# A two-layer hybrid trunk: weight sums by adding transfers, weights in blocks, adaptive sums in smaller steps

## The chip, the cores and the metric

The kernel runs on one core of a Trainium2 chip: five engines with queues of their own (TensorE, here PE, with its weight loads PEld; VectorE, DVE; ScalarE, ACT; GpSimd, POOL; SyncE, SP, which before issues every transfer) and 16 DMA engines that all transfers share. The metric is the device time of one execution in microseconds (us), as the median of several runs.

## The reference

A decoder trunk of two layers on a sequence of 1024 rows of 1024 features, then a final RMSNorm, all in float32:

```python
for l in range(DEPTH):                      # 2
    ada = c_act @ w_ada[l] + b_ada[l]       # 1024 -> 3072
    shift, scale, gate = jnp.split(ada, 3, axis=-1)
    h = rmsnorm(x, norm_g[l]) * (1.0 + scale[:, None, :]) + shift[:, None, :]
    p = h @ w_in[l]                         # 1024 -> 9224: mq, mk, mv, mo, mz, mi, mf, rq, rk, rv, rz
    ...
    cell = mlstm_chunkwise(mq_c, mk_c, mv, mi + b_igate[l], mf + b_fgate[l])      # 4 heads of 256
    y_m = jax.nn.sigmoid(mo) * head_layernorm(cell, gn_m[l], 4) * jax.nn.silu(mz)
    ret = retention_chunkwise(rq_h, rk_h, rv)                                      # 4 heads of 256
    y_r = head_layernorm(ret, gn_r[l], 4) * jax.nn.silu(rz)
    x = x + gate[:, None, :] * (jnp.concatenate([y_m, y_r], axis=-1) @ w_out[l])
return rmsnorm(x, final_g)
```

The adaptive row `ada` depends on the conditioning vector alone. The projection `h @ w_in` is most of the work.

## The kernel before

Each layer goes through a border stage (adaptive gains, the normalised input in transposed form, the first column blocks, gate logits and values of head 0), a stage of four mLSTM heads, a stage of four retention heads, and the output projection. In the trace layer 0's heads lie at about 100 to 850 us, layer 1's at 1150 to 1900.

Every float32 product is made of three products in a faster 32-bit form: a matrix is split into a high part (`hH`, `wH`: a cast) and a low part (`hL`, `wL`: the matrix less its high part), and `mm3` (line 688) multiplies high by high, low by high and high by low. `split` (line 911) does this for a 128x512 weight tile: a cast, mostly on ScalarE, then a subtraction on VectorE.

The projection goes two column blocks of 128 at a time (`pair`, line 934; 34 pairs a layer). Each block is halved along the 1024 input features, and the input along features and time, so a pair is a product of 2x2 matrices of halves; it is made with seven products of halves in place of eight (Strassen and Winograd's way). For that, sums of halves of the input are made once a layer (`sums_of_input`, line 1438, the forms T1 to T4), and sums of halves of the weights for each pair: with `a11, a21, a22, a12` the four 256 KB weight tiles, VectorE makes four sums of 128x512 in `pair`. A product of halves (`product`, line 918) is four times three matmuls of 128x512. The last product of a pair is carried into the next (`finish_pair`, line 925).

Weight tiles (`raw`, named `s` for the first sum) live in 6 slots `R0` to `R5` and up to 4 shared ones (`raw_slots`, line 796); their split halves (`wH`, `wL`) in 9 slots. A tile is overwritten only when its last reader is done, so a load, a sum and a split wait for each other through the slots. `block` (line 906) loads a tile on SyncE's queue; in DRAM the rows of 128 columns that it wants lie apart, so it comes in runs of 512 bytes.

The adaptive rows of later use (layer 1's shift and scale, both layers' gates) are made by jobs beside the pairs: `ada_rows` (line 780) loads eight tiles of 128x512 and adds them up on VectorE, each times a value of the conditioning vector (`aacc <- araw, cact`). A job is a generator, advanced by one step after each pair from a given pair on (line 1733); before, a step takes a whole row of eight loads.

The order of all instructions on all engines is fixed when the program is built: a list scheduler (`Program`, line 204) records every operation and places them by its own table of costs, due times and slots, and line 1892 then issues them in that order. This is why nearly every row of the profile has the line L1892 and groups are told apart by tile names. Each engine runs its queue strictly in this order, and a waiting instruction holds all behind it.

Of the kernel before, what the change touches and what calls it, by code (L numbers as in the profile page):

```python
# [3 lines left out]

# [1 line left out]

# [10 lines left out]
ALU = mybir.AluOpType  # L17
# [3 lines left out]
P = 128  # L21
# [590 lines left out]


@with_exitstack
def tile_hybrid_trunk(ctx, tc, x, xt, c, positions, w_ada, b_ada, norm_g, w_in, conv_w, conv_b,
                      b_igate, b_fgate, gn_m, gn_r, w_out, final_g, consts, out):
    nc = tc.nc
    x = x[0]
# [50 lines left out]
    def bank(cls):  # L669
        return new(cls, 512, "p" + cls)  # L670
# [107 lines left out]
                V.scalar_tensor_tensor(acc, raw, cact[:, kk:kk + 1], acc, ALU.mult, ALU.add)  # L778

    def ada_rows(l, c0):  # L780
        acc = new("raw", 512, "aacc", slots=raw_slots())
        raws = []
        for k in range(KT):
            raw = new("raw", 512, "araw", slots=raw_slots())
            Q.dma_start(raw, w_ada[l, k * P:(k + 1) * P, c0:c0 + 512])
            raws.append(raw)
        ada_acc(acc, raws)
        return acc

    def column_sums(pt, acc, at=0):  # L790
# [5 lines left out]
    def raw_slots():  # L796
        return R_TAGS + E_TAGS[0:{"border": 1, "ml": 4, "ret": 0}[phase[0]]]

    def ada_column_job(l, half):
        part = small("adap", 4, "s2")  # L800
        yield
        acc = ada_rows(l, half * 512)
        pt = bank("p")
        column_sums(pt, acc)
        V.tensor_copy(part, pt[:, 0:4])
        yield
        acc = ada_rows(l, D + half * 512)
        pt = bank("p")
        column_sums(pt, acc)
        finish_gsh(l, half * 4, 4, part, pt[:, 0:4])  # L810

    def gate_col_job(l):
        for half in range(2):
            acc = ada_rows(l, 2 * D + half * 512)
# [4 lines left out]
            yield  # L819

    def gate_row_job(l):
        for half in range(2):
            acc = ada_rows(l, 2 * D + half * 512)
# [12 lines left out]
            Q.dma_start(gbdr[half], g)  # L836
            yield
# [73 lines left out]
    def split(src):  # L911
# [6 lines left out]
    def product(pt, w, form, first, last):  # L918
        for k in range(4):
            cs = slice(k * P, (k + 1) * P)  # L920
            mm3(pt, (w[0][:, cs], w[1][:, cs]), forms[form][k], first and k == 0, last and k == 3, skip_group_check=True)

    carried = [None]

    def finish_pair():
        if carried[0] is None:
            return
        pX, a22, x2, done = carried[0]
        carried[0] = None
        product(pX, split(a22), "T4", False, True)  # L930
        copy(x2[0], pX)
        done()

    def pair(c1, c2, lead, done1, done2, last=False):
        a11, a21, a22 = block(c1, 0), block(c2, 0), block(c2, 1)
        s1 = new("raw", 512, "s1", slots=raw_slots())
        pX, pW = bank("p"), None
        product(pX, split(a11), "B11", True, True)
        a = new("c", 512, "ca")
        copy(a, pX)  # L940
        V.tensor_tensor(s1, a21, a22, ALU.add)
# [24 lines left out]

        def p7():
            product(pX, w3, "T3", False, True)
            x2 = new("X", W_X, "x")
            h2 = [x2[:, lead + i * HALF:lead + (i + 1) * HALF].part(i) for i in range(2)]  # L970
            V.tensor_tensor(h2[1], pX, c, ALU.add)
            carried[0] = (pX, a22, h2, lambda: done2(x2))

        if last:
            p7()
            p3()
            finish_pair()
        else:
            p3()
            p7()  # L980
# [457 lines left out]
    def sums_of_input(hf):  # L1438
        def cut(name, srcs):
            forms[name] = []  # L1440
            for s in srcs:
                two = pair_of()
                split_to(two, s)
                forms[name].append(two)

        for k in range(4):
            combine(hf[k][0], hf[k][1], hf[k][0], ALU.subtract)
        cut("T1", [hf[k][0] for k in range(4)])
        for k in range(4):
            combine(hf[k][1], hf[k][1], hf[4 + k][1], ALU.subtract)  # L1450
        for k in range(4):
            combine(hf[4 + k][1], hf[4 + k][1], hf[k][0], ALU.subtract)
        cut("T2", [hf[4 + k][1] for k in range(4)])
        cut("T3", [hf[k][1] for k in range(4)])
        for k in range(4):
            combine(hf[4 + k][0], hf[4 + k][0], hf[4 + k][1], ALU.subtract)
        cut("T4", [hf[4 + k][0] for k in range(4)])

    def plain_forms():
# [10 lines left out]
    def logit_weights(l):  # L1470
        gr = new("c", 64, "gr")
        Q.dma_start(gr.rearrange("p (k g) -> p k g", k=KT),
                    w_in[l, :, OFF_I:OFF_I + 8].rearrange("(k p) g -> p k g", p=P))
        return gr

    def value_weights(l, gr, res, k2s):
        for k2 in k2s:
            raw = new("raw", 512, "vraw", slots=raw_slots())
            Q.dma_start(raw.rearrange("p (a b) -> p a b", a=2),
                        w_in[l, k2 * 2 * P:(k2 + 1) * 2 * P, OFF_MV:OFF_MV + HD].rearrange("(a p) b -> p a b", p=P))  # L1480
            for a in range(2):
                k = 2 * k2 + a
                w = new("vw", HD + 8, "vwH", F32R), new("vw", HD + 8, "vwL", F32R)
                split_to([t[:, 0:HD].part("v") for t in w], raw[:, a * HD:(a + 1) * HD])
                split_to([t[:, HD:].part("g") for t in w], gr[:, k * 8:(k + 1) * 8])
                res.append(w)

# [216 lines left out]
    for l in range(DEPTH):  # L1704
# [186 lines left out]
    for op in made:  # L1891
# [3 lines left out]
ROUNDS = 8  # L1895
REPORT = None

_INS = ['x', 'xt', 'c', 'positions', 'w_ada', 'b_ada', 'norm_g', 'w_in', 'conv_w', 'conv_b', 'b_igate', 'b_fgate',
        'gn_m', 'gn_r', 'w_out', 'final_g']

_OUTS = [((1, T, D), 'float32')]
# [24 lines left out]
```

## Time and profile before

| | us |
|---|---|
| median of 3 runs | 2122.83 (2121.16 to 2123.99) |
| the profiled execution: its own time | 2123.29 |
| its span in the trace | 2121.4 |
| TensorE busy in it | 2091.6 (99%) |
| VectorE, ScalarE, GpSimd busy | 1769.5, 1096.8, 111.5 |
| bytes moved by DMA | 360.93 MB, DMA share 60.9% |

Names are the program's tiles without buffer numbers; `out<-in` says what an instruction writes and reads. In rows of groups stand count, busy time, mean ns of one, and the idle time of the engine before them with what ended it. In rows of waits stand the sum, the number and the longest. In rows of the timeline stand start and length, and in brackets the idle time ahead with what ended it. A matmul's end is modelled and overlaps the next one's start, so its length is not its cost. The windows give, for a stretch of time, each engine's busy time and count, the granted clock, the share of time that the DMA engines moved data, and GB/s.

### The profile page before, as it was taken

The numbers are of one execution on the slowest core, as the hardware profiler recorded it, in microseconds if no ns is written. First come the engines' busy times: TensorE is split into PE (matmuls) and PEld (weight loads), VectorE is DVE, ScalarE is ACT, GpSimd is POOL, SyncE is SP. The second block draws the span as 40 slices with busy tenths as digits, with TensorE's granted clock in tenths as the row PEclk, the third lists the DMA queues.
The fourth block names the chain that finished last, engine by engine and source line by source line (L and its number), as shares of the span: only waits on it lengthen the run. The fifth ranks groups of instructions, "written<-read, shape, count | busy, mean of one in ns | idle before, by whom it ended". The sixth has DMA issues, their size and how long they took to land.

```text
span 2121.4 us, 30466 instructions
## 1 busy us (share of the span) xinstructions
PE 2091.6 (99%) x10013; PEld 1743.0 (82%) x10013; DVE 1769.5 (83%) x3386; ACT 1096.8 (52%) x2017; POOL 111.5 (5%) x150
## 2 busy tenths in 40 slices
PE   6999999999999999999999999999999999999998
PEld 5888888888888888888888888888888888888886
DVE  7999999898988878867679998888998778788564
ACT  6754656566343434544556566555554444445342
POOL 0010111100000000000000010000000000000000
PEclk8999999999999999999999999999999999999999
DMA  9236476457585855978433665465666565679783
GB/s 296 69 109 162 129 188 174 123 143 188 171 232 152 217 142 146 267 259 267 160 96 84 156 160 153 111 166 130 186 173 167 121 176 133 159 208 275 215 246 98
DMA packets 552554, 360.93 MB, mean 170 GB/s; under 512 B 225203, under 2 KB 483003, under 8 KB 552397
## 3 DMA queue, kind: packets, MB, share of 16 engines
q1 hardware_dynamic: 552396, 359.00, 60.9%
q8 instruction: 79, 1.29, 0.3%
q14 instruction: 79, 0.64, 0.1%
HBM read 252.43 MB, written 106.46 MB: 169 GB/s over the span
## 4 chain that ended last, share of the span: by engine, by line
PE 88%; DVE 6%; DMA 2%; issue 1%; SPq 1%; ACT 1%; POOL 0%; POOLq 0%; DVEq 0%; ACTq 0%
PE pp L1892 66%; PE pa L1892 22%; DVE x L1892 1%; DVE wL L1892 1%; SPq L1892 1%; DMA araw<-in_w_ada_dram 1%; DVE rt L1892 1%; DVE acc L1892 1%; DMA vdr<-vt 0%; DVE raw L1892 0%; DVE st L1892 0%; DMA gdr<-x 0%; DMA vraw<-in_w_in_dram 0%; DMA qdr<-x 0%; ACT sq L1892 0%
## 5 line engine op out<-in xcount | busy, mean ns | idle before, releaser
L1892 PE MATMUL pp<-hH,wH 128*128 128x512 f32 x1968 | 780.8, 397 | 4.5 <-ACT hH L1892 3.1
L1892 PE MATMUL pp<-hH,wL 128*128 128x512 f32 x1968 | 779.2, 396 | 0.7 <-DVE wL L1892 0.7
L1892 PE MATMUL pp<-hL,wH 128*128 128x512 f32 x1968 | 778.5, 396 | 1.0 <-DVE hL L1892 1.0
L1892 PEld LDWEIGHTS pp<-hH,wH 128*128 128x128 f32 x1968 | 370.3, 188 | 84.7 <-ACT hH L1892 3.1
L1892 PEld LDWEIGHTS pp<-hH,wL 128*128 128x128 f32 x1968 | 370.1, 188 | 84.7 <-DVE wL L1892 2.3
L1892 PEld LDWEIGHTS pp<-hL,wH 128*128 128x128 f32 x1968 | 370.2, 188 | 81.5 <-DVE hL L1892 1.5
L1892 ACT CAST wH<-raw 128x512 fp32r<-128x512 f32 x411 | 251.8, 618 | 350.4 <-PE pp L1892 260.4
L1892 DVE TENSOR_TENSOR wL<-raw,wH 128x512 fp32r<-128x512 f32 x416 | 283.5, 683 | 73.3 <-PE pp L1892 63.3
L1892 DVE TENSOR_TENSOR oL<-wo,oH 128x512 fp32r<-128x512 f32 x128 | 87.8, 686 | 99.2 <-PE pa L1892 36.1
L1892 ACT CAST oH<-wo 128x512 fp32r<-128x512 f32 x128 | 79.3, 619 | 137.0 <-PE pp L1892 60.4
L1892 DVE SCALAR_TENSOR_TENSOR acc<-x,cols,acc 128x1024 f32<-128x1024 f32 x96 | 122.4, 1275 | 4.9 <-ACT acc L1892 4.7
L1892 POOL TENSOR_TENSOR rsd<-va,mhalf 128x2 f32<-128x2 f32 x64 | 59.7, 932 | 1185.4 <-DVE va L1892 953.0
L1892 PE MATMUL pa<-cf,q 128*128 128x258 f32 (+1 forms) x384 | 104.7, 380 | 0.1
L1892 ACT ACTIVATE nd<-nd,nmu,rsd 128x256 f32<-128x256 f32 x119 | 66.2, 595 | 62.8 <-DVE nmu L1892 62.2
L1892 DVE TENSOR_TENSOR raw<-raw,raw 128x512 f32<-128x512 f32 x136 | 92.3, 681 | 0.6
L1892 PEld LDWEIGHTS pa<-q,kk 128*128 128x128 f32 x512 | 75.0, 191 | 8.1 <-ACT nd L1892 0.7
L1892 PE MATMUL pa<-q,kk 128*128 128x128 f32 (+1 forms) x512 | 79.5, 301 | 0.5 <-ACT nd L1892 0.5
L1892 PEld LDWEIGHTS pa<-cf,q 128*128 128x128 f32 x384 | 69.6, 189 | 11.6 <-PE pp L1892 0.5
L1892 ACT COPY ca<-pp 128x512 f32<-128x512 f32 x68 | 39.7, 583 | 73.9 <-PE pp L1892 73.8
L1892 ACT COPY cb<-pp 128x512 f32<-128x512 f32 x67 | 39.1, 584 | 60.0 <-PE pp L1892 59.4
L1892 ACT ACTIVATE yH<-yg,cols 128x512 fp32r<-128x512 f32 x64 | 46.1, 724 | 42.7 <-DVE yg L1892 41.3
L1892 PE MATMUL pa<-v,sd 128*128 128x258 f32 (+1 forms) x160 | 63.0, 394 | 0.0
(250 smaller groups left out, 3694.7 us busy)
## 6 DMA issues: line engine op xcount, KB each, us to landing
raw<-in_w_in_dram SPq DMA_DIRECT2D x280, 256.0 KB
wo<-in_w_out_dram SPq DMA_DIRECT2D x128, 256.0 KB
araw<-in_w_ada_dram SPq DMA_DIRECT2D x96, 256.0 KB
qdr<-acc SPq DMA_DIRECT2D x32, 512.0 KB
kk<-qdr SPq DMA_DIRECT2D x64, 256.0 KB
q<-qdr SPq DMA_DIRECT2D x64, 256.0 KB
ndr<-zt SPq DMA_DIRECT2D x128, 128.0 KB
qdr<-x SPq DMA_DIRECT2D x32, 512.0 KB
```

What stands on the lines that cost most here:

```text
L1892: getattr(engines[op.eng], op.fn)(*[real(v) for v in op.a], **{n: real(v) for n, v in op.k.items()})
```

## The change

Four things change. The weights `w_in` are handed over in another layout, in which each 128-column block's half lies in DRAM as one 128x512 piece (rows of 2 KB), with the eight gate columns apart as `w_gate`. The four sums of a pair are made by transfers that add the incoming block onto the tile that is there (`block_added`), issued by GpSimd; each block of the sums is so read from DRAM again. For this the signs in the seven products are set anew, so that all weight sums are plain additions: the forms of the input in `sums_of_input` and three results take the signs. And the adaptive sums give way after every four loads, start with the fifth pair (layer 0) and the seventh (layer 1), and run one after another.

```diff
     def ada_rows(l, c0):
-        acc = new("raw", 512, "aacc", slots=raw_slots())
-        raws = []
+        acc = new("raw", 512, "aacc", slots=R_TAGS)
         for k in range(KT):
             raw = new("raw", 512, "araw", slots=raw_slots())
             Q.dma_start(raw, w_ada[l, k * P:(k + 1) * P, c0:c0 + 512])
-            raws.append(raw)
-        ada_acc(acc, raws)
+            if k:
+                V.scalar_tensor_tensor(acc, raw, cact[:, k:k + 1], acc, ALU.mult, ALU.add)
+            else:
+                V.tensor_scalar(acc, raw, cact[:, 0:1], None, ALU.mult)
+            if k % 4 == 3:
+                yield
         return acc
...
     def halves(col, h):
-        return w_cur[0][h * HALF:(h + 1) * HALF, col:col + P].rearrange("(a p) b -> p a b", p=P)
+        return w_cur[0][(col if col < OFF_I else col - 8) // P, h]
...
     def block(col, h):
         raw = new("raw", 512, "raw", slots=raw_slots())
-        Q.dma_start(raw.rearrange("p (a b) -> p a b", a=4), halves(col, h))
+        Q.dma_start(raw, halves(col, h))
         return raw
...
+    def block_added(raw, col, h):
+        G.dma_start(raw, halves(col, h), accum_op=ALU.add)
+        return split(raw)
...
         product(pX, split(a22), "T4", False, True)
-        copy(x2[0], pX)
+        scaled(x2[0], pX, -1.0)
         done()
 
     def pair(c1, c2, lead, done1, done2, last=False):
         a11, a21, a22 = block(c1, 0), block(c2, 0), block(c2, 1)
-        s1 = new("raw", 512, "s1", slots=raw_slots())
-        pX, pW = bank("p"), None
+        pX = bank("p")
         product(pX, split(a11), "B11", True, True)
         a = new("c", 512, "ca")
         copy(a, pX)
-        V.tensor_tensor(s1, a21, a22, ALU.add)
         pW = bank("p")
-        product(pW, split(s1), "T1", True, True)
+        product(pW, block_added(a21, c2, 1), "T1", True, True)
         c = new("c", 512, "cc")
         copy(c, pW)
         finish_pair()
-        V.tensor_tensor(a21, a21, a11, ALU.subtract)
-        V.tensor_tensor(a11, s1, a11, ALU.subtract)
-        product(pX, split(a11), "T2", False, True)
+        product(pX, block_added(a21, c1, 0), "T2", False, True)
...
-        V.tensor_tensor(a12, a12, a11, ALU.subtract)
-        w4 = split(a12)
-        w3 = split(a21)
+        w4 = block_added(a21, c1, 1)
+        w3 = block_added(a11, c2, 0)
...
-            V.tensor_tensor(h2[1], pX, c, ALU.add)
+            V.scalar_tensor_tensor(h2[1], pX, -1.0, c, ALU.mult, ALU.subtract)
...
         if l == 0:
-            jobs += [(2, rotary_job()), (18, ada_column_job(1, 0)), (21, ada_column_job(1, 1)), (26, gate_col_job(0))]
+            jobs += [(2, rotary_job()), (5, chain(ada_column_job(1, 0), ada_column_job(1, 1), gate_col_job(0)))]
         else:
-            jobs += [(18, gate_row_job(1))]
+            jobs += [(7, gate_row_job(1))]
```

Not shown: `value_weights` and `logit_weights` read the new layout, and `kernel` makes it on the host from the inputs.

The scheduler places everything anew. Three places show how. GpSimd's queue, at the turn of layer 1's mLSTM and retention heads, before (`rsd` are reciprocal roots of an attention step, `dm` its masks):

```order
L1892 AFFINE_SELECT dm_16035<-dm_16035 128x256
L1892 AFFINE_SELECT dm_16035<-dm_16035 128x128
L1892 TENSOR_TENSOR rsd_16300<-va_16290,mhalf_72 128x2
L1892 TENSOR_TENSOR rsd_16524<-va_16517,mhalf_72 128x2
L1892 TENSOR_TENSOR rsd_16644<-va_16622,mhalf_72 128x2
```

and of the change, at the same place:

```order
L1895 AFFINE_SELECT dm_16056<-dm_16056 128x128
L1895 DMA raw_15803<-in_w_in_dram 128x512
L1895 DMA raw_15872<-in_w_in_dram 128x512
L1895 TENSOR_TENSOR rsd_16383<-va_16376,mhalf_72 128x2
L1895 DMA raw_16354<-in_w_in_dram 128x512
L1895 DMA raw_15872<-in_w_in_dram 128x512
L1895 TENSOR_TENSOR rsd_16460<-va_16453,mhalf_72 128x2
L1895 DMA raw_16202<-in_w_in_dram 128x512
L1895 DMA raw_16354<-in_w_in_dram 128x512 x2
```

The adding transfers now stand between the roots. The tile raw_16354 is added to three times, and between two of these its split must have been read. ScalarE's queue a little later, before (a cast to `wH` begins a split; `ca`, `cb`, `cc` and `x` are results copied out):

```order
L1892 CAST wH_16678<-raw_16496 128x512
L1892 ACTIVATE nd_16557<-nd_16557,nmu_16672,rsd_16644 128x256
L1892 CAST wH_16688<-raw_16398 128x512
L1892 COPY cc_16694<-pp_16654 128x512
L1892 CAST wH_16713<-raw_16585 128x512
L1892 COPY x_16636<-pp_16372 128x512
L1892 COPY cb_16737<-pp_16627 128x512
L1892 CAST wH_16744<-s_3737_16717 128x512
```

and of the change:

```order
L1895 CAST wH_16489<-raw_16202 128x512
L1895 ACTIVATE x_16409<-pp_16004 128x512
L1895 COPY cb_16518<-pp_16403 128x512
L1895 CAST wH_16524<-raw_16354 128x512
L1895 CAST wH_16540<-raw_16080 128x512
L1895 CAST wH_16581<-raw_16354 128x512
L1895 CAST wH_16588<-raw_16476 128x512
L1895 COPY ca_16612<-pp_16584 128x512
L1895 COPY cc_16628<-pp_16610 128x512
L1895 CAST wH_16633<-raw_16354 128x512
```

The casts of sums made on VectorE (`s`) are gone; three casts read one tile, each after another transfer. VectorE's queue in layer 0: an adaptive sum (`aacc`) before stands among the rotations of the retention heads (`rx`, `rot`):

```order
L1892 SCALAR_TENSOR_TENSOR aacc_6240<-araw_6253,cact_102,aacc_6240 128x512
L1892 TENSOR_TENSOR x_6211<-x_6211,rot_5065 128x512
L1892 SCALAR_TENSOR_TENSOR aacc_6240<-araw_6270,cact_102,aacc_6240 128x512
L1892 TENSOR_TENSOR x_6211<-x_6211,rx_6200 128x1024
L1892 SCALAR_TENSOR_TENSOR aacc_6240<-araw_6286,cact_102,aacc_6240 128x512
L1892 STREAM_TRANSPOSE rx_6200<-x_6211 128x6x4x32
L1892 SCALAR_TENSOR_TENSOR aacc_6240<-araw_6292,cact_102,aacc_6240 128x512
```

and now stands, wider apart, among the convolutions (`acc`) of the mLSTM heads:

```order
L1895 SCALAR_TENSOR_TENSOR aacc_2183<-araw_2425,cact_102,aacc_2183 128x512
L1895 SCALAR_TENSOR_TENSOR acc_2391<-x_2041,acc_2391 128x1024
L1895 TENSOR_TENSOR wL_2477<-raw_2290,wH_2446 128x512
L1895 STREAM_TRANSPOSE x_2041<-acc_2391 128x6x4x32
L1895 SCALAR_TENSOR_TENSOR acc_2475<-x_2296,cols_104_268,acc_2475 128x1024
L1895 SCALAR_TENSOR_TENSOR aacc_2183<-araw_2430,cact_102,aacc_2183 128x512
L1895 TENSOR_TENSOR wL_2511<-raw_2299,wH_2498 128x512
```

The number of matmuls and of SyncE's transfers is the same as before; GpSimd issues 272 transfers more, and VectorE has 272 sums less.

More of the change, by code (lines that the diff above doesn't have):

```diff
@@ L3 @@
 from contextlib import ExitStack
+from itertools import chain
 import numpy as np
@@ L614, in tile_hybrid_trunk @@
 @with_exitstack
-def tile_hybrid_trunk(ctx, tc, x, xt, c, positions, w_ada, b_ada, norm_g, w_in, conv_w, conv_b,
+def tile_hybrid_trunk(ctx, tc, x, xt, c, positions, w_ada, b_ada, norm_g, w_in, w_gate, conv_w, conv_b,
                       b_igate, b_fgate, gn_m, gn_r, w_out, final_g, consts, out):
@@ L801, in ada_column_job @@
         yield
-        acc = ada_rows(l, half * 512)
+        acc = yield from ada_rows(l, half * 512)
         pt = bank("p")
@@ L806, in ada_column_job @@
         yield
-        acc = ada_rows(l, D + half * 512)
+        acc = yield from ada_rows(l, D + half * 512)
         pt = bank("p")
@@ L813, in gate_col_job @@
         for half in range(2):
-            acc = ada_rows(l, 2 * D + half * 512)
+            acc = yield from ada_rows(l, 2 * D + half * 512)
             pt = bank("p")
@@ L818, in gate_col_job @@
                             cols[l][0][:, 120 + 4 * half:124 + 4 * half].part("a"), ALU.add)
-            yield
     def gate_row_job(l):
         for half in range(2):
-            acc = ada_rows(l, 2 * D + half * 512)
+            acc = yield from ada_rows(l, 2 * D + half * 512)
             brow = new("c", 512, "brow")
@@ L836, in gate_row_job @@
             Q.dma_start(gbdr[half], g)
-            yield
     def copy(dst, src, wait=1.0):
@@ L1446, in sums_of_input @@
         for k in range(4):
-            combine(hf[k][0], hf[k][1], hf[k][0], ALU.subtract)
+            V.tensor_tensor(hf[k][0], hf[k][0], hf[k][1], ALU.subtract)
         cut("T1", [hf[k][0] for k in range(4)])
         for k in range(4):
-            combine(hf[k][1], hf[k][1], hf[4 + k][1], ALU.subtract)
+            V.tensor_tensor(hf[k][1], hf[4 + k][1], hf[k][1], ALU.subtract)
         for k in range(4):
-            combine(hf[4 + k][1], hf[4 + k][1], hf[k][0], ALU.subtract)
+            V.scalar_tensor_tensor(hf[4 + k][1], hf[4 + k][1], -1.0, hf[k][0], ALU.mult, ALU.subtract)
         cut("T2", [hf[4 + k][1] for k in range(4)])
@@ L1455, in sums_of_input @@
         for k in range(4):
-            combine(hf[4 + k][0], hf[4 + k][0], hf[4 + k][1], ALU.subtract)
+            V.scalar_tensor_tensor(hf[4 + k][0], hf[4 + k][0], -1.0, hf[4 + k][1], ALU.mult, ALU.subtract)
         cut("T4", [hf[4 + k][0] for k in range(4)])
@@ L1472, in logit_weights @@
         Q.dma_start(gr.rearrange("p (k g) -> p k g", k=KT),
-                    w_in[l, :, OFF_I:OFF_I + 8].rearrange("(k p) g -> p k g", p=P))
+                    w_gate[l].rearrange("(k p) g -> p k g", p=P))
         return gr
@@ L1478, in value_weights @@
             raw = new("raw", 512, "vraw", slots=raw_slots())
-            Q.dma_start(raw.rearrange("p (a b) -> p a b", a=2),
-                        w_in[l, k2 * 2 * P:(k2 + 1) * 2 * P, OFF_MV:OFF_MV + HD].rearrange("(a p) b -> p a b", p=P))
+            c = slice((k2 % 2) * 256, (k2 % 2 + 1) * 256)
+            Q.dma_start(raw.rearrange("p (m b) -> p m b", m=2),
+                        w_in[l, OFF_MV // P:OFF_MV // P + 2, k2 // 2].rearrange("m p b -> p m b")[:, :, c])
+            by_row = raw.rearrange("p (m a b) -> p a m b", m=2, a=2)
             for a in range(2):
@@ L1483, in value_weights @@
                 w = new("vw", HD + 8, "vwH", F32R), new("vw", HD + 8, "vwL", F32R)
-                split_to([t[:, 0:HD].part("v") for t in w], raw[:, a * HD:(a + 1) * HD])
+                split_to([t[:, 0:HD].part("v").rearrange("p (m b) -> p m b", m=2) for t in w], by_row[:, a])
                 split_to([t[:, HD:].part("g") for t in w], gr[:, k * 8:(k + 1) * 8])
@@ L1896 @@
 REPORT = None
-_INS = ['x', 'xt', 'c', 'positions', 'w_ada', 'b_ada', 'norm_g', 'w_in', 'conv_w', 'conv_b', 'b_igate', 'b_fgate',
+_INS = ['x', 'xt', 'c', 'positions', 'w_ada', 'b_ada', 'norm_g', 'w_in', 'w_gate', 'conv_w', 'conv_b', 'b_igate', 'b_fgate',
         'gn_m', 'gn_r', 'w_out', 'final_g']
@@ L1910 @@
     arrays, args = {}, []
+    w = inputs['w_in']
+    tiles = _np.concatenate([w[:, :, :OFF_I], w[:, :, OFF_I + 8:]], axis=2).reshape(DEPTH, 2, 4, P, -1, P)
+    inputs = dict(inputs, w_in=tiles.transpose(0, 4, 1, 3, 2, 5).reshape(DEPTH, -1, 2, P, 4 * P),
+                  w_gate=w[:, :, OFF_I:OFF_I + 8], xt=inputs['x'][0].T)
     for name in _INS:
-        a = _np.ascontiguousarray(inputs['x'][0].T if name == 'xt' else inputs[name])
+        a = _np.ascontiguousarray(inputs[name])
         arrays[f"in_{name}_dram"] = a
```

## The prediction

> **What bounds the kernel now.** I read the page first: the busy shares and the slices.
>
> ```profile
> PE 2091.6 (99%) x10013; PEld 1743.0 (82%) x10013; DVE 1769.5 (83%) x3386; ACT 1096.8 (52%) x2017; POOL 111.5 (5%) x150
> PEclk8999999999999999999999999999999999999999
> ```
>
> TensorE is busy for 99% of the span at full granted clock, but matmul durations overlap, so that share alone cannot tell how full it is. The windows can: from 100 to 150 us TensorE runs nothing but 128x512 products.
>
> ```profile
> core 0: us, PE busy (x) PEld busy (x) DVE busy (x) ACT busy (x) POOL busy (x), PEclk, DMA share, GB/s
> 0.00:60.00 60.00, 41.65 (x239) 37.60 (x240) 44.61 (x109) 40.08 (x89) 3.21 (x8) 0.89 0.82 265
> 60.00:2113.00 2053.00, 2049.65 (x9776) 1705.37 (x9774) 1721.96 (x3274) 1054.50 (x1925) 107.16 (x140) 1.00 0.61 167
> 2113.00:2121.40 8.40, 0.29 (x2) 0.00 (x0) 2.96 (x6) 2.17 (x4) 1.08 (x2) 0.66 0.49 187
> 100.00:150.00 50.00, 50.00 (x217) 40.47 (x216) 49.56 (x67) 28.49 (x41) 7.93 (x5) 1.00 0.32 91
> 100.00:850.00 750.00, 747.07 (x3568) 620.97 (x3567) 673.14 (x1325) 387.40 (x719) 51.92 (x61) 1.00 0.60 161
> 1150.00:1900.00 750.00, 749.58 (x3564) 624.33 (x3563) 645.57 (x1202) 389.05 (x723) 38.89 (x60) 1.00 0.58 154
> ```
>
> 217 products in 50.00 us are 0.2304 us each: that is the pitch of a TensorE that never waits. In the whole body (60 to 2113 us) it idles 2053 - 2049.65 = 3.35 us. Some waits hide under the modelled end of the matmul before, so the weight loads are the stricter witness; their waits in 60 to 2110 us, largest first:
>
> ```profile
> PEld pp L1892 <- ACT wH L1892: 2.3, 2, 1.2
> PEld pp L1892 <- DVE wL L1892: 2.3, 4, 1.1
> PEld pa L1892 <- issue: 1.3, 4, 0.6
> PEld pa L1892 <- ACT nd L1892: 1.0, 2, 0.7
> PEld pp L1892 <- DVE aL L1892: 0.5, 1, 0.5
> ...
> ```
>
> With six further rows of 0.3 to 0.5 us all of them come to 9.8 us. The change takes no product away (same count, same sizes), so in 2053 us of body there are between 3.35 and 9.8 us to win; the 18.4 us that TensorE idles in the first 60 us are another matter, and the 8 us tail is untouched. VectorE at 83% is not the bound.
>
> **Part 1: sums leave VectorE.** These rows go (136 + 68 + 68 = 272 instructions, four for each of 68 pairs of column blocks), and the last one is replaced by a SCALAR_TENSOR_TENSOR:
>
> ```profile
> L1892 DVE TENSOR_TENSOR raw<-raw,raw 128x512 f32<-128x512 f32 x136 | 92.3, 681 | 0.6
> L1892 DVE TENSOR_TENSOR raw<-s,raw 128x512 f32<-128x512 f32 x68 | 46.4, 682 | 0.2
> L1892 DVE TENSOR_TENSOR s<-raw,raw 128x512 f32<-128x512 f32 x68 | 46.3, 681 | 2.5 <-DMA raw<-in_w_in_dram 2.5
> L1892 DVE SCALAR_TENSOR_TENSOR aacc<-araw,cact,aacc 128x512 f32<-128x512 f32 x80 | 59.5, 743 | 2.1 <-DMA araw<-in_w_ada_dram 1.7
> L1892 DVE TENSOR_TENSOR x<-pp,cc 128x512 f32<-128x512 f32 x68 | 46.0, 677 | 0.6 <-PE pp L1892 0.6
> ```
>
> 92.3 + 46.4 + 46.3 = 185.0 us leave; 68 x (743 - 677) ns = 4.5 us come. VectorE falls from 1769.5 to about 1589 us. Nearly all of that lies beside TensorE and is worth nothing; what it can free is part of the 3.35 to 9.8 us.
>
> **Part 2: the adaptive sums move.** The two worst places of the body lie in the stage (560 to 720 us) where before makes four of these sums, eight loads each (the first two rows are windows with the columns above, the others single matmuls with their start and length):
>
> ```profile
> 590.00:595.00 5.00, 4.20 (x18) 2.65 (x18) 4.72 (x10) 2.09 (x4) 0.00 (x0) 1.00 1.03 348
> 688.00:695.00 7.00, 5.67 (x27) 3.83 (x26) 6.41 (x11) 2.97 (x7) 0.00 (x0) 1.00 0.98 287
> 594.10 0.51 PE L1892 MATMUL pp<-hH,wH 128*128 128x512 f32 x1 [0.80 <-ACT wH L1892]
> 690.19 0.50 PE L1892 MATMUL pp<-hH,wL 128*128 128x512 f32 x1 [0.67 <-DVE wL L1892]
> 693.44 0.51 PE L1892 MATMUL pp<-hH,wH 128*128 128x512 f32 x1 [0.66 <-ACT wH L1892]
> ```
>
> There VectorE and the DMA engines are full and TensorE waits for splits: 0.80 + 1.33 = 2.13 us of its 3.35. The steps are now spread from the fifth pair on, four loads and four multiply-adds a pair: 4 x 743 ns = 3.0 us of VectorE, against 4 x 681 ns = 2.7 us taken away by part 1, so the earlier stage keeps its load and should not get worse. I count the whole 3.35 us as won by parts 1 and 2 (bounds: 0, if other waits take their place, and 9.8).
>
> **Part 3: blocks laid out in one piece.** A 256 KB block comes as 128 runs of 2 KB, no longer 512 of 512 bytes. No row prices that alone; per 256 KB (0.262 MB) the start needs 0.96 x 50 us x 0.262 MB / (312 GB/s x 50 us) = 0.81 us of all sixteen engines, the pair stages 0.60 x 0.262 / 0.161 = 0.98 us:
>
> ```profile
> 0.00:50.00 50.00, 32.04 (x172) 28.96 (x173) 34.61 (x89) 30.08 (x73) 2.26 (x8) 0.86 0.96 312
> raw<-in_w_in_dram SPq DMA_DIRECT2D x280, 256.0 KB
> ```
>
> I take the difference, 0.17 us a block (bounds 0 and twice that). It is hidden except at the start, where the DMA engines are at 96% and TensorE waits for loads: four blocks, 0.7 us.
>
> **Part 4: 272 transfers that add, on GpSimd's queue.** This is the unknown: the trace of before has none. The tile of the third block now goes through load, add, split, add, split, add, split, where the next add must wait for the split's second half. For each add I counted in the new order how much TensorE work lies between the product that frees the split's slots and the first product of the split that the add feeds, at 0.2304 us a product. That is the time it may take: 60 or 61 products, 13.8 to 14.1 us, are the commonest, half of the adds have over 16.9 us; of 272, 68 have under 14 us, 23 under 12, 11 under 10, the least 7.8 us. What it needs: a cast and its second half, the issue, the landing, a cast:
>
> ```profile
> L1892 ACT CAST wH<-raw 128x512 fp32r<-128x512 f32 x411 | 251.8, 618 | 350.4 <-PE pp L1892 260.4 <-DVE raw L1892 66.3 <-DMA raw<-in_w_in_dram 11.7
> L1892 DVE TENSOR_TENSOR wL<-raw,wH 128x512 fp32r<-128x512 f32 x416 | 283.5, 683 | 73.3 <-PE pp L1892 63.3 <-ACT wH L1892 2.6 <-PE pa L1892 2.3
> L1892 POOL TENSOR_TENSOR rsd<-va,mhalf 128x2 f32<-128x2 f32 x64 | 59.7, 932 | 1185.4 <-DVE va L1892 953.0 <-ACT cf L1892 64.2 <-DVE v L1892 52.5
> 608.81 0.38 SPq L1892 DMA_DIRECT2D raw<-in_w_in_dram  x1
> 614.52 0.62 ACT L1892 CAST wH<-raw 128x512 fp32r<-128x512 f32 x1 [1.09 <-DMA raw<-in_w_in_dram]
> 939.67 3.13 SPq L1892 DMA_DIRECT2D wo<-in_w_out_dram  x2
> 941.94 0.62 ACT L1892 CAST oH<-wo 128x512 fp32r<-128x512 f32 x1 [2.19 <-DMA wo<-in_w_out_dram]
> ```
>
> A plain 256 KB load was used 614.52 - 608.81 = 5.71 us after its issue in a busy stage, 941.94 - 939.67 = 2.27 us in a quiet one. For the issue I take GpSimd's dearest small operation, 0.93 us (an estimate; the affine selects beside it are shorter). Sum: 0.62 + 0.68 + 0.93 + 5.71 + 0.62 = 8.6 us, and about 1.2 us (chosen, not measured) for hand-overs and engines that are not free: 9.8 us. Adding up what the shorter budgets lack, counting only chains that do not overlap, gives 1.1 us at a need of 9.5 us, 3.8 at 10, 8.8 at 10.5, 30 at 12, 70 at 14; I take 2.5. Below nothing it cannot go, since an add removes no wait of its own; the upper end I take at a need of 12 us, a landing of 7.9. GpSimd itself has room: 272 x 0.93 = 253 us on top of 111.5 in 2121. What stands behind a waiting add on its queue are other adds, the reciprocal roots of the attention (the normalise step) and the masks; for a root the least budget counted the same way is 5.2 us and the median 11.3, before 4.8 and 11.1, so the waiting costs nothing unless an add is late by several us.
>
> The Trainium skill ("DMA: Bandwidth & Descriptors", Anatomy of one DMA — SWDGE (gpsimd) path) fits a transfer issued by GpSimd with about 2.0 us plus bytes over 436 GB/s, which makes 2.6 us here as an estimate; by that the need is 6.7 us, no budget falls short and part 4 costs nothing. No run here shows such a transfer yet; the plain ones in this trace took 2.3 to 5.7 us.
>
> **The sum,** against the profiled execution's own 2123.3 us (span 2121.4 and 1.9 around it; the median of the runs shown is 2122.8, 0.5 lower): -0.7 (start) - 3.35 (waits of the body) + 2.5 (short budgets) = **2121.7 us**. That is no change: about 0.2%, 4.2 us, is what a measurement of this kernel can tell from none.
>
> **Rivals.** *The adds land late* (slower). Mechanism: an add that reads its destination and writes it back takes longer than a load, and three in series on one tile eat the 13.8 us. It decides from a need of 10.5 us, where the shortfalls (8.8 us) exceed the 4.05 us won by more than 4.2; at 12 us the kernel takes 2121.7 - 2.5 + 30 = 2149 us. For it: the loads of a busy stage already need 5.7 us. Against it: 249 of 272 budgets exceed 12 us. *The DMA engines fill* (slower). The adds bring 272 x 0.81 to 272 x 1.95 us (the second end: twice 0.98, two streams read) into 1500 us of pair stages: 0.60 becomes 0.72 (after part 3's 0.03) to 0.92 on average, and the 560 to 720 us stage, 0.72 on average, would be over 1 at the upper end: some 5% of 160 us, 8 us, 2127 us. *The adds land early and the freed VectorE ends the waits* (faster). Then the 9.8 us go with the 0.7: 2112.8 us at best, half of it 2118. For it: the budgets' median of 16.9 us. Against: waits on attention results and issue are in the 9.8 and not touched. *It does not matter at all*: waits move elsewhere; 2122.6 us, inside the forecast.
>
> **Chances.** Forecast and the rival of no effect, both within 0.2%: 0.42. Late adds 0.26, full DMA engines 0.05: slower 0.31. Early adds: faster 0.27. The range runs from just over the floor, 2113.5, to a need of 12 us, 2150; of the late adds some 0.13 lies above it, of the early ones 0.03 below.
>
> **What will show it.** Part 1: the raw and s rows gone, VectorE near 1589 us. Part 2: no TensorE waits near 590 and 690 us. Part 3: the first 60 us with TensorE idling 17.7 us in place of 18.4. Part 4: waits of the casts for transfers of the third tile short, weight loads waiting under 10 us in all. Wrong would be: a body in which TensorE idles tens of us before products of the summed blocks (late adds), DMA shares over 0.95 in the pair stages, or a pitch other than 0.2304 us.

## The result and the profile after

The changed kernel takes **2157.36 us** (median of 4 runs, 2153.85 to 2160.32) against 2123.14 for the kernel before beside it (4 runs, 2121.16 to 2123.99): a ratio of 1.0162, 95% interval 1.0143 to 1.0181. It is 34.2 us slower, and outside the forecast's range. The profiled execution took 2153.85 us; its span is 2152.1, 30.7 longer than before's 2121.4. First the page's busy times and GpSimd's DMA queue (packets, MB, share of sixteen engines):

```profile
PE 2103.8 (98%) x10013; PEld 1747.0 (81%) x10013; DVE 1619.6 (75%) x3121; ACT 1081.8 (50%) x2010; POOL 340.3 (16%) x422
...
q0 software_dynamic: 39168, 71.32, 20.8%
```

Then windows of it, with the columns as before:

```profile
0.00:60.00 60.00, 43.84 (x250) 39.61 (x251) 43.06 (x106) 39.70 (x89) 3.92 (x9) 0.89 0.83 270
60.00:2143.00 2083.00, 2058.95 (x9762) 1706.88 (x9761) 1573.02 (x3010) 1039.43 (x1917) 335.25 (x411) 1.00 0.78 199
150.00:250.00 100.00, 90.52 (x403) 73.32 (x401) 91.92 (x188) 47.34 (x91) 16.95 (x22) 0.95 0.84 203
560.00:720.00 160.00, 159.44 (x750) 132.01 (x749) 109.63 (x193) 65.14 (x127) 30.01 (x34) 1.00 0.83 199
```

In the body TensorE idles 2083 - 2058.95 = 24.1 us in place of 3.35; in the first 60 us it idles 16.2 in place of 18.4. That is 18.5 us more idle time. The other 12.2 us of the span are in TensorE's busy time, 2103.8 in place of 2091.6 for the same 10013 matmuls. Waits that hide under modelled ends are most of them: the waits of the weight loads in the body, 9.8 us before, sum to 38.6, so some 14.5 us hide in place of 6.4. A lower granted clock can be the rest (0.95 over the worst 100 us, 150 to 250, where before had 1.00; 0.992 in the mean, before 0.995).

The adds (q0, GpSimd's queue) take 20.8% of sixteen engines for 2152.1 us: 1.65 us for each of 272. What TensorE waited for in the body, the largest first (sum, count, longest):

```profile
PE pa L1895 <- ACT sd L1895: 5.3, 5, 1.9
PE pa L1895 <- DVE T L1895: 5.0, 1, 5.0
PE pp L1895 <- ACT wH L1895: 3.4, 2, 2.2
PE pa L1895 <- DMA kk<-qdr: 2.0, 3, 1.2
PE pp L1895 <- ACT aH L1895: 1.9, 1, 1.9
PE pa L1895 <- DVE dm L1895: 1.8, 1, 1.8
PE pa L1895 <- ACT nd L1895: 1.6, 3, 0.7
```

The same view of ScalarE, its casts' wait for weight transfers:

```profile
ACT wH L1895 <- DMA raw<-in_w_in_dram: 184.2, 94, 5.6
```

Little of it is a product that waits for its own split (`wH`, 3.4 us). Most is attention and gates (`sd`, `T`, `kk`, `dm`, `nd`), which use no weight sum. (The `dm` row is not the adds' doing: the kernel e5 below, which has none, waits 1.8 us for it too.) But ScalarE's casts now stand 184.2 us waiting for weight transfers, where before they stood 11.7. The chain of waits between 1746 and 1766 us shows how the one becomes the other (start, length, what):

```profile
1746.06 5.75 DMA raw<-in_w_in_dram
1751.81 0.02 issue
1751.83 0.63 ACT wH L1895
1752.46 0.02 issue
1752.48 0.70 DVE wL L1895
1753.19 0.39 issue
1753.58 7.71 DMA raw<-in_w_in_dram
1761.29 0.02 issue
1761.32 0.63 ACT wH L1895
1761.94 0.02 issue
1761.97 0.69 DVE wL L1895
1762.66 0.33 DVE sr L1895
1762.99 1.13 DVE x L1895
1764.12 0.21 DVE sr L1895
1764.34 0.02 issue
1764.36 0.52 ACT sd L1895
1764.88 0.04 issue
1764.93 0.50 PE pa L1895 x2
```

An add, the two halves of its split, the next add on the same tile, its split: 16.6 us for two steps. VectorE waits in `wL`; behind that stands `sr`, a mask times an attention result that does not need the weights, then ScalarE's cast `sd` and TensorE's product with it, which waited 1.20 us. Here the late tile is paid for by what stands behind it in the queues. It is one of the slow adds: the median from issue to landing is 5.3 us.

### The profile page after: what moved, and what is told of

It is laid out like the page before. It is cut to its first block, busy times and chain, and to the rows that moved or that the text cites. A ratio compares the mean times of both kernels' runs of the same rounds, so it can differ in the third digit from the quotient of the medians.

```text
span 2152.1 us, 30927 instructions
## 1 busy us (share of the span) xinstructions
PE 2103.8 (98%) x10013; PEld 1747.0 (81%) x10013; DVE 1619.6 (75%) x3121; ACT 1081.8 (50%) x2010; POOL 340.3 (16%) x422
## 3 DMA queue, kind: packets, MB, share of 16 engines
q0 software_dynamic: 39168, 71.32, 20.8%
## 5 line engine op out<-in xcount | busy, mean ns | idle before, releaser
L1895 ACT CAST wH<-raw 128x512 fp32r<-128x512 f32 x474 | 288.1, 618 | 392.4 <-PE pp L1895 196.8
L1895 DVE TENSOR_TENSOR wL<-raw,wH 128x512 fp32r<-128x512 f32 x484 | 327.2, 684 | 175.8 <-ACT wH L1895 109.6
L1895 POOL DMA_DIRECT2D raw<-in_w_in_dram x272 | 239.1, 905 | 1169.5 <-DVE wL L1895 567.1
L1895 DVE STREAM_TRANSPOSE zt<-nd 128x512 f32<-128x512 f32 x64 | 45.2, 707 | 41.4 <-ACT nd L1895 38.5
L1895 POOL TENSOR_TENSOR rs<-s,mhalf 128x1 f32<-128x1 f32 (+1 forms) x12 | 10.1, 853 | 362.3 <-DVE s L1895 326.2
```

The costliest lines, as they stand in the source:

```text
L1895: getattr(engines[op.eng], op.fn)(*[real(v) for v in op.a], **{n: real(v) for n, v in op.k.items()})
```

## The experiments

Three theories. **A**: the adds end too late for the order; the casts waiting for them hold ScalarE and VectorE with the attention's work behind. **B**: the adaptive sums, moved into the stage where the worst stalls now are (150 to 250 us), cause them. **C**: the DMA engines' load, 0.78 in place of 0.61, slows every transfer. Times are medians, ratios are to the kernel before on the same chip, with 95% intervals.

### The parts of the change, one without the other

Four kernels made of the diff's parts: layout alone (`halves`, `block`, `value_weights`, `w_gate`); steps alone (`ada_rows` and the jobs); both without adds; layout and adds without the steps. In the first three `pair` stays as before.

> The kernel before with the blocks laid out in pieces (2 KB runs) and nothing else: the four sums of a pair stay on VectorE, the adaptive sums stay in whole rows. Theory A (the adding transfers end later than the order was planned for, and the cast that waits for one holds ScalarE's queue with the attention's work behind it): nothing of the loss is here, ratio 0.996 to 1.000, 2115 to 2123 us, since 280 loads each cost some 0.17 us less of the DMA engines. Theory B (the adaptive sums, now among the mLSTM heads, cause the stalls between 150 and 250 us): the same, 2115 to 2123. Theory C (the DMA engines' load, 0.78 in the body after, slows every transfer): the same, at a DMA share of 0.57 or 0.58.

> The kernel before with the adaptive sums in smaller steps and from the fifth or seventh pair on, and nothing else. Theory A: no loss, 2118 to 2124 us; the forecast's own part 2 says 1 to 3 us less than before. Theory B: the stalls between 150 and 250 us (about 12 us of TensorE there in the profile after) come with it, 2130 to 2140. Theory C: some of it, 2122 to 2128, since the bytes are the same and only stand elsewhere.

> Layout and smaller steps, the sums on VectorE: the changed kernel without its adding transfers. Theory A: the whole loss is gone, 2115 to 2122 us, VectorE near 1770. Theory B: 2130 to 2140. Theory C: 2115 to 2122, at a DMA share of 0.58.

> Layout and adding transfers, the adaptive sums in whole rows from the 18th pair on as before. Theory A: the loss stays, 2148 to 2165 us, with the worst place moved from 150-250 to 560-720 us, where the adaptive loads come on top of the adds. Theory B: 2125 to 2135. Theory C: 2145 to 2160, most of it in 560-720 us where the DMA share comes near 1.

| | us | ratio |
|---|---|---|
| layout alone | 2125.89 | 1.0010 (1.0001 to 1.0019) |
| steps alone | 2126.41 | 1.0011 (1.0002 to 1.0020) |
| layout and steps | 2126.56 | 1.0012 (1.0003 to 1.0021) |
| layout and adds | 2180.32 | 1.0264 (1.0239 to 1.0288) |

All three without adds lie 0.1% over before, 2 to 5 us above what A expected, and none gains; the loss is the adds'. B falls: with the old steps the adds cost even more, 56 us, more than any theory expected. About half of the 22 us on top of the adds' 34 lies where the adaptive loads now meet the adds (TensorE busy 148.95 of 160 us between 560 and 720, at a clock of 0.96, against 159.44 in the changed kernel). Yet B has a grain of truth. Two windows of the kernel before:

```profile
150.00:250.00 100.00, 99.79 (x457) 81.58 (x456) 99.25 (x203) 51.34 (x95) 4.32 (x3) 1.00 0.58 156
560.00:720.00 160.00, 157.88 (x764) 130.61 (x764) 138.92 (x252) 64.34 (x124) 5.09 (x5) 1.00 0.72 201
```

and of the steps alone:

```profile
150.00:250.00 100.00, 96.15 (x426) 78.23 (x425) 98.82 (x186) 50.53 (x90) 0.54 (x2) 0.98 0.59 164
560.00:720.00 160.00, 160.00 (x769) 133.63 (x768) 127.83 (x226) 70.82 (x134) 3.92 (x5) 1.00 0.59 158
```

The 2.1 us of idle time at 560 to 720 us are won, as forecast, and 3.6 us are lost at 150 to 250, where VectorE was already at 99%.

### What an add does beyond a load

The same instructions in the same order, but each of the 272 transfers overwrites its tile:

```diff
-        getattr(engines[op.eng], op.fn)(..., **{n: real(v) for n, v in op.k.items()})
+        getattr(engines[op.eng], op.fn)(..., **{n: real(v) for n, v in op.k.items() if n != "accum_op"})
```

> The changed kernel, every instruction in the same place, but the 272 transfers of GpSimd overwrite their tile in place of adding onto it, so the products use single blocks where sums should be. It parts what an add costs the DMA engines (1.65 us of all sixteen by the profile after, 0.81 for a plain 256 KB load) from the chain of load, split, transfer, split on one tile, which stays. Theory A, that the chain is too long as such: the landing hardly shortens, 2145 to 2157 us. Theory A with the add's own time as its cause, and theory C too: the landing falls by 0.8 us or more and the DMA share in the body from 0.78 to 0.68, so most of the loss goes, 2122 to 2132 us.

**2123.65 us, ratio 1.0004 (0.9995 to 1.0014)**: the whole loss is gone. The page's row of GpSimd's queue in this run:

```profile
q0 software_dynamic: 21760, 71.32, 11.0%
```

The view of the weight tile: GpSimd's issues (ns, min/median/max), and all its transfers' time from issue to landing:

```profile
L1895 POOL DMA_DIRECT2D raw<-in_w_in_dram x272: 536/538/1056, 50.1 to 1900.5; - x136
...
DMA to landing us min/median/max: 2.6/3.6/7.5
```

The same view of the changed kernel:

```profile
L1895 POOL DMA_DIRECT2D raw<-in_w_in_dram x272: 844/870/1539, 51.2 to 1928.8; - x136
...
DMA to landing us min/median/max: 3.7/5.3/8.8
```

A window of e5:

```profile
60.00:2100.00 2040.00, 2034.96 (x9693) 1693.29 (x9692) 1568.20 (x2996) 1044.86 (x1907) 245.67 (x409) 1.00 0.68 203
```

and of the changed kernel:

```profile
60.00:2100.00 2040.00, 2015.95 (x9576) 1672.00 (x9575) 1554.06 (x2979) 1026.72 (x1891) 334.17 (x409) 1.00 0.79 202
```

ScalarE's wait for weight tiles in e5, 184.2 us with the adds:

```profile
ACT wH L1895 <- DMA raw<-in_w_in_dram: 33.2, 28, 4.3
```

For the same bytes an add lands 1.7 us later (5.3 in place of 3.6, counted from the start of the issue), its issue takes 0.3 us more, and it costs the engines 1.65 in place of 0.86 us (11.0% of 2123.3 over 272). Neither the chain of dependences nor the extra bytes (both have some 200 GB/s) nor the order costs anything that shows, with plain loads in the adds' place. And with VectorE 147 us less busy the time is still before's: the freed engine is worth nothing that shows.

### Later, or more load?

To e5 a delay is added, on GpSimd ahead of each transfer, that waits for the tile as the transfer does:

```diff
+        if "accum_op" in op.k:
+            nc.gpsimd.memset(real(op.a[0])[:, 0:1], 0.0)                                  # e11
+            nc.gpsimd.tensor_tensor(real(op.a[0])[:, 0:1], real(ones), real(mhalf)[:, 0:1], ALU.pow)   # e12; twice in e7
```

or, behind each transfer, load that nobody waits for:

```diff
+        if "accum_op" in op.k:
+            nc.gpsimd.dma_start(spare[turn % 4], real(op.a[1]))    # e8; behind every second one in e13
+            turn += 1
```

> e5_plain_loads (the 272 transfers overwrite their tile, so single blocks stand where sums should be), with two small power operations of GpSimd, some 0.7 us each, on the first column of the tile ahead of each of them: they wait for the tile's readers as the transfer does, so the chain of load, split, transfer, split gets about 1.5 us longer, as long as that of the adds (4.83 us from issue to landing in the median after, 3.22 in e5), while the DMA engines keep e5's load, 0.68 in the body. If it is the length of the chain that costs (theory A): 2145 to 2165 us. If it is the DMA engines' load, which slows all the other transfers (theory C): 2122 to 2130 us.

> e5_plain_loads with another transfer behind each of the 272, issued by GpSimd, of the same 256 KB block from DRAM into a spare tile in DRAM that nobody reads: the DMA engines get about the load of the adds or more (0.78 to 0.82 in the body), and the chain stays as in e5 but for what the load itself does to it. Theory A: 2123 to 2130 us. Theory C: 2145 to 2165 us.

> e7's delay and e8's spare transfers together: chain and load of the adds, without an add. If these two are all that an add does, the time is near the changed kernel's: 2150 to 2170 us; if the sum of e7's and e8's losses is clearly less than this one's, they need each other.

> e5_plain_loads with one memset of GpSimd on the first column of the tile ahead of each of the 272 transfers: a chain longer by some 0.5 us (0.1 for the memset, 0.4 of hand-over as in e7's rows) at e5's load of the DMA engines. Where the length of the chain costs from small amounts on (a straight line from e5 to e7: 118 us for 2.06): 2145 to 2155 us. Where a chain has some room left: 2123 to 2130.

> e5_plain_loads with one power operation ahead of each transfer: a chain longer by some 1.2 us. A straight line gives 2185 to 2200 us, a curve that begins flat and turns up 2135 to 2165. An adding transfer's landing is 1.6 us later than a plain one's and its issue is held 0.3 us longer, so if the lengthened chain alone is the cause, this run has to cost about as much as the adds: over 2145.

> e8_load_behind with a spare transfer behind every second of the 272 only: a DMA share of about 0.72 to 0.73 in the body. In proportion between e5 (2123.7 at 0.68) and e8 (2154.3 at 0.77): 2137 to 2141 us. If the load costs only from a share above 0.7 on: 2124 to 2132.

| | added to a transfer | DMA share 60-2100 us | us | ratio |
|---|---|---|---|---|
| e5 | nothing | 0.68 | 2123.65 | 1.0004 (0.9995 to 1.0014) |
| e11 | 0.53 us of delay | 0.70 | 2125.01 | 1.0009 (1.0000 to 1.0018) |
| e12 | 1.3 us | 0.69 | 2158.52 | 1.0172 (1.0157 to 1.0187) |
| e7 | 2.1 us | 0.66 | 2242.04 | 1.0554 (1.0534 to 1.0573) |
| e13 | load, every second | 0.74 | 2131.08 | 1.0034 (1.0022 to 1.0046) |
| e8 | load | 0.77 | 2154.33 | 1.0147 (1.0131 to 1.0162) |
| e9 | 2.1 us and load | 0.70 | 2330.83 | 1.0975 (1.0958 to 1.0991) |

The median landings that e7's expectation gives, 4.83 and 3.22 us, are not those of the views above, 5.3 and 3.6; the difference is nearly the same. The delays are worked out from groups of GpSimd's rows (busy time, mean ns of one | idle time before): the operation and the hand-over to the transfer, 0.91 + 110/272 = 1.3 us in e12, of which these are the rows:

```profile
L1896 POOL TENSOR_TENSOR raw<-ones,mhalf 128x1 f32<-128x1 f32 x272 | 247.9, 911 | 924.2 <-DVE wL L1897 521.5 <-ACT cb L1897 148.3 <-ACT wH L1897 88.2
L1897 POOL DMA_DIRECT2D raw<-in_w_in_dram x272 | 159.1, 585 | 109.9 <-POOL raw L1896 105.0 <-DMA raw<-in_w_in_dram 2.0 <-DVE mv L1897 0.8
```

So half a microsecond is free, 1.3 us cost 35, 2.1 cost 118: the shape that theory A's budgets have, flat and then steep. But load alone costs 30 us too, with a landing of 4.3 us only, and half of it 8. The issue of a spare transfer also holds GpSimd's queue, for 0.51 us by its rows; e11 holds it about as long, ahead of the transfer, and loses 2 us, so this is unlikely to be what costs in e8. ScalarE's waits for weight tiles, in e12:

```profile
ACT wH L1897 <- DMA raw<-in_w_in_dram: 151.6, 83, 6.6
```

324.1 us in e7; in e8, and there also a wait of TensorE's that only load brings:

```profile
ACT wH L1896 <- DMA raw<-in_w_in_dram: 105.0, 66, 6.1
```

```profile
PE pa L1896 <- DMA kk<-qdr: 4.0, 5, 1.4
```

TensorE waits directly for the attention's `kk` in e8 (4.0 us) and in the changed kernel (2.0), not in e12 or before: an add brings both marks, the late tile and the slowed transfers of others. The two are not additive: e9 loses 207 us where e7 and e8 lose 118 and 30. Nor is a delay quite a late landing: delays stand one behind another in GpSimd's queue, while landings overlap, and e7 and e9 come out far over the 2145 to 2165 and 2150 to 2170 us that were expected, e9 at six times the adds' loss. That the queueing of the delays is the reason is not shown, and e12 may overshoot too. So an add costs by coming late, by its load, or by both, and each made alone here costs about as much as the adds; how the 34 us divide is open.

### Can another order hide it?

The scheduler's costs of an add are set near the trace: its service time doubled, 3.0 us in place of 1.5 from its end to its reader.

```diff
+            add = 1 if op.k.get("accum_op") is not None else 0
...
+            op.serve *= 1 + add
...
-                    t1 = op.end + (0.5 if op.pin else self.FAR if op.far else self.LATE * (2 if o.eng == "PE" else 1))
+                    t1 = op.end + (0.5 if op.pin else self.FAR if op.far else self.LATE * (2 if o.eng == "PE" or op.eng == "POOL" else 1))
```

> The changed kernel, with the scheduler's costs of an adding transfer set nearer to the trace: twice the service time of a plain load (1.62 us) and 3.0 us in place of 1.5 between its end and its reader. Theory A in its form that the order was planned with too short adds, so that casts stand too early in ScalarE's queue: most of the loss comes back, 2125 to 2135 us. If the chain of adds is too long for 9 split slots and the tiles there are, however it is planned, or theory C holds: 2140 to 2160 us.

**2160.5 us, ratio 1.0180 (1.0165 to 1.0195)**: no better. Its waits are of another kind, on ScalarE:

```profile
ACT wH L1897 <- DMA raw<-in_w_in_dram: 19.9, 12, 5.4
```

and on TensorE:

```profile
PE pp L1897 <- DVE wL L1897: 14.1, 13, 2.4
PE pp L1897 <- ACT wH L1897: 8.9, 5, 2.5
```

Planned with truer times ScalarE hardly waits for the tiles any more (19.9 us in place of 184.2), and now the products themselves wait for their splits. The wait moves from the queues to the tile. So the form of theory A that only the plan was at fault falls for this scheduler; that the chain has no room for three such adds in any order, with these slots, is not shown.

### Fewer adds, and adds that do not follow one another

e10 makes only the first sum of a pair by an add; e14 all four, in every second pair; e15 two sums in each pair, alone on their tiles:

```diff
 # e10
-        product(pX, block_added(a21, c1, 0), "T2", False, True)
+        V.tensor_tensor(a21, a21, a11, ALU.add)
+        product(pX, split(a21), "T2", False, True)
...
-        w4 = block_added(a21, c1, 1)
-        w3 = block_added(a11, c2, 0)
+        V.tensor_tensor(a12, a12, a21, ALU.add)
+        w4 = split(a12)
+        V.tensor_tensor(a21, a21, a22, ALU.subtract)
+        w3 = split(a21)
 # e15, against e10
-        V.tensor_tensor(a21, a21, a22, ALU.subtract)
-        w3 = split(a21)
+        w3 = block_added(a11, c2, 0)
```

> The changed kernel with only the first sum of each pair made by an adding transfer (68 adds, one on a tile), the other three on VectorE (the fourth as the third tile's sum less a22). Theory A, the chain of three adds on one tile: the loss is gone, 2120 to 2128 us. Theory C, in proportion to the adds: a quarter of the 35 us, 2130 to 2135 us; if the load only costs once the engines are near full: 2122 to 2128.

> The changed kernel with the four adding transfers in every second pair only (136 of 272; the other pairs make their sums on VectorE, with the change's signs): the chain of three adds on one tile is whole where it is made, and the DMA share is about 0.69 in the body. If the chain as such costs: half the loss, 2135 to 2145 us. If the adds cost by their load and that only counts beyond a share of about 0.7: 2121 to 2130.

> The changed kernel with two of the four sums of a pair made by adding transfers, each alone on its tile (the first sum on the third block's tile, the last on the first block's), and the two sums between them on VectorE: 136 adds as in e14_half_pairs and the same load of the DMA engines, 0.69 to 0.70 in the body, but no add waits for the split of a sum that another add made. If it is the adds in series on one tile that cost: no loss, 2120 to 2127 us. If it is their load or the single landing: as e14, 2133 to 2140 us.

e10: 2122.35 us, 0.9996 (0.9987 to 1.0006). e14: 2136.18, 1.0067 (1.0050 to 1.0083). e15: 2128.02, 1.0021 (1.0012 to 1.0031). From 60 to 2100 us the DMA share is 0.70 in e14 and in e15. ScalarE's wait for weight tiles in e14:

```profile
ACT wH L1908 <- DMA raw<-in_w_in_dram: 62.9, 45, 4.0
```

The same of e15:

```profile
ACT wH L1897 <- DMA raw<-in_w_in_dram: 16.4, 13, 2.6
```

With the same 136 adds and the same load, 0.70, adds in series lose 12.9 us and adds alone on their tiles 5.0, a little over what was expected of them, and the cast's waiting falls from 62.9 to 16.4 us. The series is the likely cause of these 7.9 us, but not the only difference: e14 also has its adds four to a pair in every second pair, e15 two in each, and both orders are planned anew. The 5 us left are for load, landing and order together. With 68 adds nothing is lost, and nothing won: no version here is faster than the kernel before.

## Why the prediction was wrong

**The bound** was right: TensorE's pitch bounds the kernel, and VectorE does not. In e5 VectorE is as free as after the change, the adds' price is away, and the time is before's. That is also the end of the rival "adds land early": even then nothing is won. And "it does not matter at all" holds for the change without its adds only.

**Part 1** is right in kind, off in size: VectorE fell to 1619.6 us, not 1589. The rows' 681 ns overlap with the next instruction's start. Two pieces of the chain of waits in the steps-alone run (start, length, what) show a first sum and one of the others at what they hold of VectorE:

```profile
205.73 0.60 DVE s L1894
...
206.93 0.60 DVE raw L1894
```

272 x 0.60 = 163 us, and 150 are measured. The 4.5 us that the scaled results were to cost did not come: their rows hold 46.2 us in place of 46.0, so a price taken from the row of `aacc` did not fit them. Copies and casts that came over from ScalarE (5 `x`, 4 `cc`, 5 `wH`) hold some 8 us in the rows; the last few are not accounted for. Part 1 had no effect on the time.

**Part 2** won what it said at 560 to 720 us, and the sentence that the earlier stage "should not get worse" failed: steps alone, where VectorE has no sums taken away, lose 3.6 us there, and in e5, where they are taken away, it is still 3.35 idle (96.65 of 100 us). So the -3.35 us of the sum came to nothing: e5's body idles 2040 - 2034.96 = 5.0 us.

**Part 3** held at its place: layout alone idles 17.3 us in the first 60, for a forecast of 17.7 (before 18.4). A block saved 0.13 us of the engines in place of 0.17 (60.9% of 2121.4 us before, 59.0% of 2126.9 with layout alone, over 280 blocks). It is not seen in the total: the same kernel's body idles some 4 us more after a new planning, and all three of the parts without adds came 0.1% over before.

**Part 4 is the step that failed**: the term of 2.5 us for short budgets, which came out as the whole loss of 34, since the rest of the change costs and wins nothing (e5). The need was not the fault. It was put at 9.8 us with 6.64 for issue and landing together; measured is a median of 5.3 from the start of the issue (GpSimd's instruction 0.905 us, forecast 0.93, though that was not its dearest small operation: a root of 128x4 took 1.18), so by the same sum the need is 8.4 us. By the counted budgets (1.1 us at 9.5) that costs next to nothing. The spread does not mend it: a tenth of the adds landed after more than 7.2 us, a need of 10.4, and if all did, the count would give less than 8.8 us. The delays say the same without an add: by the same sum e11, e12 and e7 need 7.5, 8.1 and 8.8 us, and they lost 2, 35 and 118.

What was wrong is the price of a need, in two places. The count asked only whether the product fed by an add comes too late, and looked for what is held only on GpSimd's queue (the roots). It left out that the cast and the subtraction that wait for the add stand in ScalarE's and VectorE's queues, ahead of attention work: 184.2 us of ScalarE's waiting, and a TensorE that waits mostly for `sd`, `T`, `kk` and `nd` (5.3, 5.0, 2.0 and 1.6 us; in e5, without adds, 0, 0.9, 0 and 0.2). And it took chains that don't overlap as independent, where one add's lateness starts the next (the pair at 1746 us; e15 against e14, as far as that goes). Beside the price of a need, the load of the adds stood in the sum at nothing, and load alone cost 30 us in e8. Which part of the 34 us is whose stays open, as said above.

**The rivals.** "Adds land late" named the mechanism, but put its point of decision at a need of 10.5 us; the loss was there at a need of about 8.4, so that its 2149 us came near was luck: it was worked out from a need of 12 that the median add did not have. "The DMA engines fill" had the load right (0.81 to 1.95 us an add, measured 1.65; a share of 0.72 to 0.92, measured 0.79) and the price wrong: it charged only the part over a share of 1, 8 us at most, whereas in e8 a mean share of 0.77 cost 30 us without any add.

The Trainium skill ("DMA: Bandwidth & Descriptors", Anatomy of one DMA — SWDGE (gpsimd) path) makes 2.6 us for a 256 KB transfer of GpSimd, as an estimate by its fit. The quickest plain one in e5 took just that, 2.6 us; the median was 3.6, and of the adds 5.3, the quickest 3.7. In this kernel it is where the plain transfers begin, not what they take, and the forecast that part 4 costs nothing by it was further off than the one by the rows.

## What to carry to other kernels

Price a late operand by everything that stands behind its reader in an in-order queue, not by that reader's own consumer alone; the sum of an engine's waits for transfers (ScalarE: 11.7 to 184.2 us) is a sign of it. It is no measure: the replanned kernel had 19.9 us of it and lost as much. Work moved from an engine that isn't the bound onto a resource that is shared by all, here the DMA engines, bought nothing and had its price in other engines' queues. A twin kernel in the same order, with the suspected property alone taken away (e5), showed in one run that the adding itself was the cause, which the parts of the diff could not.

## What the runs showed of the hardware

An adding transfer of 256 KB took 1.9 times the DMA engines' time of a plain one on the same queue, 1.65 against 0.86 us of all sixteen, for the same bytes, and in smaller pieces: 39168 packets in place of 21760 for 272 transfers. The Trainium skill ("DMA: Bandwidth & Descriptors", Rules for kernel authors) says that an accumulate reads its destination and writes it later; nearly twice the engines' time fits that, though no row here shows the reads apart. Bytes per second therefore hide this load: 202 and 203 GB/s in the windows of the two kernels, at shares of 0.79 and 0.68. And mean shares well under 1 were felt here: with spare transfers behind every one of the loads the kernel lost 1.5% at a mean of 0.77, behind every second one 0.3% at 0.74.
